# Operand addresses, whole-chunk 32-row products and a first expert without them, in a one-layer diffusion block with a mixture of experts

## The chip, the cores and the metric

The kernel runs on one core of one Trainium2 chip. TensorE (PE) multiplies matrices and loads its stationary operand by separate weight loads (PEld); VectorE (DVE), ScalarE (ACT) and GpSimd (POOL) work on elements; SyncE (SP) issues the large transfers. The metric is the time in device microseconds of one execution. It is compared with the time of the kernel before, as the median of several executions.

## The reference

One layer over 1024 latent tokens and 256 context tokens of width 1024. First a token mixer (a gated MLP over chunks of 128 tokens and a gated linear attention, fed by one input projection, merged and projected out), then a mixture of 16 experts, of which each token takes 2 out of one group of 4. Cut to what matters here:

```python
def moe_ffn(h, w_router, b_router, w_g, w_u, w_d):
    logits = h.astype(jnp.float32) @ w_router.astype(jnp.float32) + b_router.astype(jnp.float32)
    probs = jax.nn.softmax(logits, axis=-1).reshape(n_tok, N_EXPERT_GROUPS, EXPERTS_PER_GROUP)
    group_score = lax.top_k(probs, TOP_K)[0].sum(-1)
    g_sel = jnp.argmax(group_score, axis=-1)
    in_group = jnp.take_along_axis(probs, g_sel[:, None, None], axis=1)[:, 0]
    top_w, top_i = lax.top_k(in_group, TOP_K)
    weight = top_w / jnp.sum(top_w, axis=-1, keepdims=True)
    expert = (g_sel[:, None] * EXPERTS_PER_GROUP + top_i).reshape(-1).astype(jnp.int32)
```

Each expert computes (silu(h w_g) * (h w_u)) w_d on its tokens, with an inner width of 1536; the result, times the token's weight and a gate, is added to the stream, and a last RMSNorm follows. The inputs and weights are fp32.

## The kernel before

**Products.** An fp32 product is made from three fp32r ones: each operand is split into a high part (a copy rounded by ScalarE) and a low part (the rest, by VectorE), and hi·hi, hi·lo and lo·hi are added up in PSUM. So a matmul of 128x128 by 512 columns appears three times, with names ending in h and l.

**Stages.** The input projection (mm<-hxh,wh and the like, L256), the attention, the gate and branch projections (mm<-gbh and mm<-zh, L256), the output projection (L994), the router, and from about 1160 us on the experts.

**Experts.** The experts are handled in an order sorted by their counts, in 16 slots; RANK tells which of the sorted experts stands in which slot, and the first slot always holds expert 0. Each slot has room for 128 tokens in the block "a" and for 32 times UNITS[slot] tokens more in the block "b". An expert has 18 weight pages of 1 MB: three chunks of 4 for gate and up (w_gu) and 6 for down (w_d). load() has SP bring a page into one of ten raw buffers; part() has ScalarE and VectorE split it into one of three hl buffers; block_a() runs 12 matmuls of 512 columns per page from hl, with the stationary xah, xal (the tokens, transposed) or aah, aal (the activations). block_b() uses the raw fp32 page and 32 stationary columns, four products side by side in the array, for two pages at a time: 16 instructions with one unit, 32 with two. They are recorded as twice as many. After each chunk silu and a product on ScalarE and VectorE make sa (and sb_ for block b), PE transposes them (aat, abt), and split_a() makes aah and aal.

**Around the experts.** own_rows() finds the tokens of the first expert, and its rows are gathered by POOL as soon as they are known. places() works out the tokens of all other slots, on VectorE, behind the first chunk of the first expert. The rows of the next expert are gathered in the second chunk. At the end of a slot ya (and yb) is added to the stream in memory by an indirect transfer of POOL (put). In the last slot, tail() fetches finished rows (fetched, tile fx) and normalises them (normed, tile fq) while the last expert runs. If an expert has more tokens than its slot has room for, a loop behind the last slot handles the rest in blocks (overflow_block), with the expert's pages loaded again.

**Order.** Each engine works through its instructions in a fixed order. The program's scheduler sets it from the order of the code and from issue_after, which lets instructions be issued only behind a named one.

Of the kernel before, what the change touches and what calls it, by code (L numbers as in the profile page):

```python
# [18 lines left out]
S = 1024  # L19
D = 1024  # L20
CT = 256
E = 16
# [31 lines left out]
UNITS = tuple(2 if r == 1 else 1 if r < 10 else 0 for r in RANK)  # L54
# [24 lines left out]
def constants():  # L79
    p = np.arange(128)  # L80
    s, t = p[:, None], p[None, :]
    f = np.concatenate([
        np.eye(128),
        np.ones((128, 128)),
        (s < t) * 1.0,
        (s % 32) == np.arange(2),
    ], 1).astype(np.float32)
    t64 = np.arange(64)[None, :]
    i = np.concatenate([
        (s % 64) <= t64, (s % 64) >= t64,  # L90
        2 * (s + 128 * (np.arange(16) // 2)[None, :]) + (np.arange(16) % 2)[None, :],
        np.broadcast_to(2 * (S + np.arange(CAP) % TRASH)[:, None], (CAP, 16)).reshape(128, 144),
    ], 1).astype(np.int32)
# [12 lines left out]
    sl[:, 3] = 15 - e + 65536 * (e == 0)  # L106
    c = np.arange(128)[None, :]
    g4, r = s // 32, s % 32
    trash = np.concatenate([S + s, 4 * (S + 128 + r) + g4, 4 * (S + 160 + r) + g4], 1)
    z = np.concatenate([  # L110
        np.broadcast_to(16 * np.concatenate([c, 128 + c % 32, 160 + c % 32], 1), (128, 384)),
        np.broadcast_to([[32, 128, 128]], (128, 3)), np.broadcast_to([[1, 4, 4]], (128, 3)),
        np.concatenate([0 * s, g4, g4], 1) - trash, trash,
        np.stack([s // 32 + 4 * np.arange(8)[None], np.broadcast_to(s % 32, (128, 8)), np.ones((128, 8)),
                  np.zeros((128, 8))], 2).reshape(128, 32),
    ], 1).astype(np.float32)
    return f, i, g.reshape(128, 96), ((s - t) % 32 == 0).astype(np.float32), z, sl.reshape(128, 64)
# [48 lines left out]
def body(tc, A, out):  # L166
# [39 lines left out]
    sil = cp.tile([128, 8, 2], F32, name="sil")  # L206

# [737 lines left out]
    tk0, ch0 = (cp.tile([128, 3], I32, name=n) for n in ("tk0", "ch0"))  # L945
# [27 lines left out]
    kz = t1.tile([128, 428], F32, name="kz")  # L973
# [11 lines left out]
    V.tensor_copy(tri.rearrange("p i c -> p (i c)"), kz[:, 396:428])  # L985
# [142 lines left out]
    def own_row(i):  # L1128

        R = st_[i][5]  # L1130
        V.tensor_scalar(own[:, i, :], kz[:, 0:384], R[:, 7, 0:1], R[:, 5, 0:1], op0=ALU.is_equal, op1=ALU.mult)
        V.tensor_copy(tri[:, i, 3:4], R[:, 4, 0:1])

    def own_rows():

        p = ax("own")
        for b in range(3):
            for i in range(8):
                PE.matmul(p[:, 4 * b:4 * b + 4], own[:, i, 128 * b:128 * b + 128], tri[:, i, :], start=i == 0,
                          stop=i == 7)  # L1140
        f = t1.tile([128, 3, 4], F32, name="f3")
        V.tensor_copy(f.rearrange("p b c -> p (b c)"), p[:, 0:12])
        for c in range(3):
            V.tensor_mul(f[:, :, c], f[:, :, c], kz[:, 384 + 3 * c:387 + 3 * c])
        V.tensor_add(f[:, :, 0], f[:, :, 0], f[:, :, 1])
        V.tensor_add(f[:, :, 2], f[:, :, 2], kz[:, 393:396])
        V.tensor_add(f[:, :, 0], f[:, :, 0], f[:, :, 2])
        placed.append(V.tensor_copy(tk0, f[:, :, 0]))
        V.tensor_copy(ch0, f[:, :, 3])
# [10 lines left out]
    raws, ready = [], []  # L1160
# [17 lines left out]
    def load():  # L1178
        raws.append(page_tile([128, 2048]))
        e, n, i = order.pop(0)  # L1180
        return SP.dma_start(raws[-1], A[n][bass.ds(expert(e), 1), i].rearrange("o p n -> (o p) n") if e else A[n][0, i])

    def part():
        raw = raws.pop(0)
        hl = split_tile()
        SC.activation(hl[:, 0, :], raw, AF.Copy)  # L1186
        V.tensor_sub(hl[:, 1, :], raw, hl[:, 0, :].bitcast(F32))  # L1187
        ready.append(tuple(a.rearrange("p (k n) -> p k n", k=2) for a in (raw, hl[:, 0, :], hl[:, 1, :])))

    def page():  # L1190
        if not ready:
            if not raws:
                load()
            part()
        return ready.pop(0)
# [84 lines left out]
    with tc.issue_after(counted.ins), tc.issue_after(scaled.ins):  # L1280
        for i in range(2):
            part()
# [61 lines left out]
    x1_quarter = x1_d.rearrange("t (g c) -> (t g) c", g=4)  # L1344
    zf = ep_.tile([128, 512], F32, name="zf", tag="fq", bufs=FQB)
# [14 lines left out]
    def block_a(acc, st, k0, pg, start, stop):  # L1360

        _, wh, wl = pg
        for k in range(2):
            for n, (x, w) in enumerate(((0, wh), (0, wl), (1, wh))):
                for h in range(2):
                    PE.matmul(acc[h], st[x][:, k0 + k, :], w[:, k, 512 * h:512 * h + 512],  # L1366
                              start=start and (k, n) == (0, 0), stop=stop and (k, n) == (1, 2))

    def block_b(n, acc, st, k0, pgs, first, last):

        if n > 1 and first:
            PE.matmul(acc, zz[:, 0:128], zz, start=True, stop=False)
        for i, (w, _, _) in enumerate(pgs):
            for j in range(n):
                for k in range(2):
                    end = last and (i, j, k) == (len(pgs) - 1, n - 1, 1)
                    for g in range(4):
                        PE.matmul(acc[32 * g:32 * g + 32, 256 * j:256 * j + 256], st(j, k0 + 2 * i + k),
                                  w[:, k, 256 * g:256 * g + 256], start=n == 1 and first and (i, k) == (0, 0), stop=end,
                                  tile_position=(0, 32 * g))  # L1380
# [165 lines left out]
    wAB = prep_a(0, *first_xa, ch0[:, 0:1]), prep_b(0, first_xb[0], lambda j: ch0[:, j + 1:j + 2])  # L1546
    before = []
    for e in range(E):
        U = UNITS[e]
        for c in range(3):  # L1550
            pa, pb = [pt(f"pa{h}", "pa", 4) for h in range(2)], pt("pb", "pb", 2) if U else None
            for i in range(0, 4, 2):
                pgs = [page() for k in range(2)]
                first = e + c + i == 0
                if not first:
                    block_b(U, pb, xb_, 2 * i, pgs, i == 0, i == 2)
                for k in range(2):
                    block_a(pa, XA, 2 * (i + k), pgs[k], i + k == 0, i + k == 3)
                if first:
                    block_b(U, pb, xb_, 2 * i, pgs, i == 0, i == 2)  # L1560
            if U:
                sb_ = ep_.tile([128, 2, 128], F32, name="sb_", bufs=2)
                pv = pb.rearrange("p (j u n) -> p j u n", j=2, u=2)[:, 0:U]
                SC.activation(sb_[:, 0:U], pv[:, :, 0], AF.Silu)
                V.tensor_mul(sb_[:, 0:U], sb_[:, 0:U], pv[:, :, 1])
            p = pt("aat", "pt", 2)
            for h in range(2):
                sa = ep_.tile([128, 2, 128], F32, name="sa", bufs=4)
                pv = pa[h].rearrange("p (g u n) -> p g u n", g=2, u=2)
                SC.activation(sa, pv[:, :, 0], AF.Silu)  # L1570
                mul = V.tensor_mul(sa, sa, pv[:, :, 1])
                for k in range(2):
                    PE.transpose(p[:, 256 * h + 128 * k:256 * h + 128 * k + 128], sa[:, k, :], ident)
            split_a(p, aah[:, 4 * c:4 * c + 4, :], aal[:, 4 * c:4 * c + 4, :])
            if U:
# [3 lines left out]
                SC.activation(abT[:, c, 0:U].rearrange("p j t -> p (j t)"), p[:, 0:128 * U], AF.Copy)  # L1579
            if c == 0:  # L1580
# [10 lines left out]
        for i in range(0, 6, 2):  # L1591
            pgs = [page() for k in range(2)]
            block_b(U, pb, ab_, 2 * i, pgs, i == 0, i == 4)
            for k in range(2):
# [54 lines left out]
    ep_.release()  # L1649
    cp.release()  # L1650
# [15 lines left out]
```

## Time and profile before

| | us |
|---|---|
| median of 3 executions | 2281.84 |
| lowest and highest | 2281.76, 2284.72 |
| the profiled execution | 2284.32 |
| its span, first to last instruction | 2282.5 |
| PE, DVE, ACT, POOL busy | 2207.9, 1417.8, 1059.9, 205.0 |

The span is the time that the trace covers; 1.8 us of the profiled execution lie around it. The mean granted clock of TensorE was 0.985 of full speed. Busy time is a union of the intervals in which an engine's instructions ran; a matmul's record is longer than the distance to the next one's start, because matmuls overlap.

### The profile page before, as it was taken

Reading aid. Unit: us, or ns where it says so; the run is one execution under the profiler, and the core shown is the slowest. Engines: PE = TensorE matmul, PEld = TensorE weight load, DVE = VectorE, ACT = ScalarE, POOL = GpSimd, SP = SyncE. Lnnn points to the kernel's source line nnn. Section 1 sums busy time; section 2 is a strip of 40 time slices with the busy share of each in tenths; the row PEclk is TensorE's granted clock in tenths of the full one; section 3 lists DMA queues with packets and bytes.
Section 4 is the critical chain, followed back from the end, with each engine's and each line's share of the span. In section 5 each row is a group of like instructions: output and inputs, shape, how many; then the busy total and the mean of one; then the engine's idle time right before and its main releaser. Section 6 shows DMA issues by size and latency. Waiting matters only on the chain. (4 is left out here: it accounts for less than half of the span.)

```text
span 2282.5 us, 36688 instructions
## 1 busy us (share of the span) xinstructions
PE 2207.9 (97%) x14595; PEld 1785.5 (78%) x14596; DVE 1417.8 (62%) x2135; ACT 1059.9 (46%) x1334; POOL 205.0 (9%) x176
## 2 busy tenths in 40 slices
PE   9999999999999999999969999999999999999975
PEld 6999898888889978888957677777777777777654
DVE  5644215846762354246877568786868687666667
ACT  3312125534542153233235456665757565555554
POOL 0011000000000000001331110000101010100031
PEclk9999999999999999999979999999999999999988
DMA  7665433656741366445658679797979798877774
GB/s 291 195 207 170 154 128 105 195 179 194 233 169 59 116 220 225 157 129 204 186 194 304 228 279 347 285 362 289 366 283 375 288 348 303 288 278 278 261 254 161
DMA packets 141986, 530.06 MB, mean 232 GB/s; under 512 B 17159, under 2 KB 57919, under 8 KB 94705
## 3 DMA queue, kind: packets, MB, share of 16 engines
q1 hardware_dynamic: 119584, 467.97, 56.2%
q0 software_dynamic: 21072, 55.43, 8.8%
q10 hardware_dynamic: 1152, 4.26, 0.5%
q8 instruction: 116, 1.90, 0.3%
q14 instruction: 62, 0.50, 0.1%
HBM read 457.36 MB, written 70.44 MB: 231 GB/s over the span
## 5 line engine op out<-in xcount | busy, mean ns | idle before, releaser
L1187 DVE TENSOR_TENSOR hl<-praw,hl 128x2048 fp32r<-128x2048 f32 x174 | 402.0, 2313 | 157.6 <-ACT hl L1186 155.1
L1366 PE MATMUL pa<-hl,xah 128*128 128x512 f32 x1536 | 437.1, 403 | 16.1 <-ACT hl L1186 11.4
L1186 ACT ACTIVATE hl<-praw 128x2048 fp32r<-128x2048 f32 x174 | 333.1, 1915 | 206.2 <-PE pa L1366 206.1
L1366 PEld LDWEIGHTS pa<-hl,xah 128*128 128x128 f32 x1536 | 284.7, 189 | 98.4 <-issue 17.3
L1187 DVE TENSOR_TENSOR hl<-raw,hl 128x2048 fp32r<-128x2048 f32 x114 | 261.0, 2291 | 114.4 <-ACT hl L1186 113.0
L1186 ACT ACTIVATE hl<-raw 128x2048 fp32r<-128x2048 f32 x114 | 218.4, 1916 | 139.2 <-PE pa L1366 135.1
L1366 PE MATMUL pa<-hl,xal 128*128 128x512 f32 x768 | 243.1, 397 | 0.0
L1366 PE MATMUL pa<-hl,aah 128*128 128x512 f32 x768 | 219.3, 403 | 5.7 <-DVE hl L1187 4.5
L256 PE MATMUL mm<-wh,hxh 128*128 128x256 f32 (+1 forms) x768 | 218.3, 284 | 4.6 <-DVE vv L285 3.5
L256 PE MATMUL mm<-wl,hxh 128*128 128x256 f32 (+1 forms) x768 | 216.6, 282 | 0.0
L256 PE MATMUL mm<-wh,hxl 128*128 128x256 f32 (+1 forms) x768 | 215.8, 281 | 0.0
L256 PE MATMUL mm<-hxh,wh 128*128 128x512 f32 x448 | 178.7, 399 | 0.0
L256 PE MATMUL mm<-hxh,wl 128*128 128x512 f32 x448 | 178.6, 399 | 0.0
L256 PE MATMUL mm<-hxl,wh 128*128 128x512 f32 x448 | 178.4, 398 | 0.0
L1366 PEld LDWEIGHTS pa<-hl,aah 128*128 128x128 f32 x768 | 141.8, 189 | 45.5 <-DVE hl L1187 5.4
L1366 PEld LDWEIGHTS pa<-hl,xal 128*128 128x128 f32 x768 | 144.1, 189 | 34.3
L256 PEld LDWEIGHTS mm<-wh,hxh 128*128 128x128 f32 x768 | 145.2, 189 | 5.6 <-DVE vv L285 3.8
L256 PEld LDWEIGHTS mm<-wl,hxh 128*128 128x128 f32 x768 | 145.3, 189 | 0.0
L256 PEld LDWEIGHTS mm<-wh,hxl 128*128 128x128 f32 x768 | 145.0, 189 | 0.0
L238 DVE TENSOR_TENSOR wl<-wraw,wh 128x2048 fp32r<-128x2048 f32 (+1 forms) x36 | 82.7, 2298 | 100.1 <-ACT wh L237 78.8
L1366 PE MATMUL pa<-hl,aal 128*128 128x512 f32 x384 | 121.6, 398 | 0.0
L237 ACT ACTIVATE wh<-wraw 128x2048 fp32r<-128x2048 f32 (+1 forms) x36 | 69.1, 1918 | 69.9 <-PE mm L256 67.7
(503 smaller groups left out, 3623.4 us busy)
## 6 DMA issues: line engine op xcount, KB each, us to landing
praw<-in_w_gu_dram SPq DMA_DIRECT2D x116, 1024.0 KB, 6.8
raw<-in_w_gu_dram SPq DMA_DIRECT2D x76, 1024.0 KB, 7.2
praw<-in_w_d_dram SPq DMA_DIRECT2D x58, 1024.0 KB, 8.1
raw<-in_w_d_dram SPq DMA_DIRECT2D x38, 1024.0 KB, 7.5
wraw<-in_w_in_dram SPq DMA_DIRECT2D x24, 1024.0 KB, 4.8
wraw<-in_w_mod_dram SPq DMA_DIRECT2D x18, 1024.0 KB, 5.7
vb<-v_d POOLq DMA_DIRECT2D x16, 1024.0 KB, 6.8
xt<-in_x_dram SPq DMA_DIRECT2D x16, 512.0 KB, 5.7
```

The source lines that it names most:

```text
L237: SC.activation(wh[:, :n], raw[:, :n], AF.Copy)
L238: V.tensor_sub(wl[:, :n], raw[:, :n], wh[:, :n].bitcast(F32))
L256: end = PE.matmul(acc, Wst[a](k), Wmv[b](k), start=n == 0, stop=n == tot - 1)
L1186: SC.activation(hl[:, 0, :], raw, AF.Copy)
L1187: V.tensor_sub(hl[:, 1, :], raw, hl[:, 0, :].bitcast(F32))
L1366: PE.matmul(acc[h], st[x][:, k0 + k, :], w[:, k, 512 * h:512 * h + 512], start=start and (k, n) == (0, 0), stop=stop and (k, n) == (1, 2))
```

## The change

It has three parts. Three unused tiles (pad_l, pad_r, pad_e) move the tiles behind them in SBUF. The first slot has no block "b": UNITS[0] is 0, so own_rows() looks for 128 rows instead of 384, and no second gather is made for it. And block_b() runs for a whole chunk at once, four pages in gate/up and three in down, ahead of block_a(); the transposes of a chunk (turned_a) are issued behind the next chunk's block_b(), or behind the first page's block_a() in slots without units; pages are split when block_a() asks for them, while block_b() takes raw pages ahead.

```diff
-UNITS = tuple(2 if r == 1 else 1 if r < 10 else 0 for r in RANK)
+UNITS = tuple(0 if r == 0 else 2 if r == 1 else 1 if r < 10 else 0 for r in RANK)
...
+    cp.tile([128, 16], F32, name="pad_l")
+    rp = tc.alloc_tile_pool(name="rp", bufs=1, side="right")
+    rp.tile([128, 24], F32, name="pad_r")
...
-    own = t1.tile([128, 8, 384], BF16, name="own")
+    own = t1.tile([128, 8, 128], BF16, name="own")
...
-        for b in range(3):
-            for i in range(8):
-                PE.matmul(p[:, 4 * b:4 * b + 4], own[:, i, 128 * b:128 * b + 128], tri[:, i, :], start=i == 0,
-                          stop=i == 7)
+        for i in range(8):
+            PE.matmul(p[:, 0:4], own[:, i, :], tri[:, i, :], start=i == 0, stop=i == 7)
...
-    first_xb = gather_b(0, lambda j: tk0[:, j + 1:j + 2])
-    with tc.issue_after(first_xb[1][-1].ins):
+    with tc.issue_after(first_xa[1].ins):
         scatter(7)
...
+    ep_.tile([128, 24], F32, name="pad_e")
...
+    def turned_a(c, sas, sb_, U, behind):
+
+        with tc.issue_after(behind.ins):
             p = pt("aat", "pt", 2)
-            for h in range(2):
...
+            for k in range(4):
+                PE.transpose(p[:, 128 * k:128 * k + 128], sas[k // 2][:, k % 2, :], ident)
             split_a(p, aah[:, 4 * c:4 * c + 4, :], aal[:, 4 * c:4 * c + 4, :])
...
+    for e in range(E):
+        U = UNITS[e]
+        left = None
+        for c in range(3):
+            pa, pb = [pt(f"pa{h}", "pa", 4) for h in range(2)], pt("pb", "pb", 2) if U else None
+            if U:
+                end = block_b(U, pb, xb_, 0, raw_pages(4), True, True)
+                if left:
+                    turned_a(*left, end)
+            for k in range(4):
+                end = block_a(pa, XA, 2 * k, page(), k == 0, k == 3)
+                if k == 0 and left and not U:
+                    turned_a(*left, end)
...
-        for i in range(0, 6, 2):
-            pgs = [page() for k in range(2)]
-            block_b(U, pb, ab_, 2 * i, pgs, i == 0, i == 4)
-            for k in range(2):
-                block_a(pa, AA, 2 * (i + k), pgs[k], i + k == 0, i + k == 5)
-            if i == 2 and e + 1 < E:
-                wAB = prep(e + 1, *nxt)
-            if e + 1 == E:
-                tail(f"d{i}")
+        for i in range(0, 6, 3):
+            if U:
+                end = block_b(U, pb, ab_, 2 * i, raw_pages(3), i == 0, i == 3)
+                if i == 0:
+                    turned_a(*left, end)
+            if i == 3 and e + 1 < E:
+                wAB = prep(e + 1, *nxt)
+            for k in range(i, i + 3):
+                end = block_a(pa, AA, 2 * k, page(), k == 0, k == 5)
+                if k == 0 and not U:
+                    turned_a(*left, end)
+                if e + 1 == E and k % 2:
+                    tail(f"d{k - 1}")
```

The order on PE at the beginning of the third gate/up chunk of the fourth slot, which has one unit: pb is block b's product, pa are block a's, aat and abt the transposes of the chunk before. Before:

```order
L1378 MATMUL pb<-raw,xbT 32x256 x16
L1573 MATMUL aat<-kf,sa 128x128 x2
L1578 MATMUL abt<-kf,sb__13367 128x128
L1366 MATMUL pa_13388<-hl,xah 128x512
L1573 MATMUL aat<-kf,sa 128x128 x2
L1366 MATMUL pa_13389<-hl,xah 128x512
```

The same place after the change:

```order
L1385 MATMUL pb<-raw,xbT 32x256 x32
L1562 MATMUL aat<-kf,sa 128x128 x4
L1567 MATMUL abt<-kf,sb__13178 128x128
L1372 MATMUL pa_13189<-hl,xah 128x512
L1372 MATMUL pa_13190<-hl,xah 128x512
```

Before, 16 products of block b alternate with 24 of block a; now 32 stand ahead of all 48 of block a, and all five transposes stand right behind them.

The order on VectorE in the first expert after its first chunk, where L1311 to L1347 are places(), hl the low halves of pages and sa the activations. Before:

```order
L1187 TENSOR_TENSOR hl<-praw,hl 128x2048
L1325 TENSOR_TENSOR w_11565<-sel,fi 128x256
L1332 CAST ids<-fo 128x48
L1571 TENSOR_TENSOR sa<-sa,pa_11632 128x256
L1326 TENSOR_REDUCE fo<-w_11565 128x16
```

After the change:

```order
L1322 TENSOR_TENSOR sel<-ks,rank 128x256
L1193 TENSOR_TENSOR hl<-praw,hl 128x2048
L1330 TENSOR_TENSOR w_11498<-sel,fi 128x256
L1427 TENSOR_TENSOR aal<-aat,aah 128x512
L1331 TENSOR_REDUCE fo<-w_11498 128x16
L1193 TENSOR_TENSOR hl<-praw,hl 128x2048
```

In both, the instructions of places() alternate with the low halves; in the order after the change they also stand ahead of and behind aal of the first chunk.

The order on ScalarE in the last expert behind its first chunk, where fq is the squared sum of a finished row block and hl the high half of a page. Before:

```order
L1570 ACTIVATE sa<-pa_19071 128x256
L1509 ACTIVATE fq,fs<-fx 128x1024
L1418 ACTIVATE aah<-aat 128x512
L1509 ACTIVATE fq,fs<-fx 128x1024
L1186 ACTIVATE hl<-raw 128x2048
```

After the change:

```order
L1592 ACTIVATE sa<-pa_18882 128x256
L1517 ACTIVATE fq,fs<-fx 128x1024 x2
L1192 ACTIVATE hl<-raw 128x2048
L1521 ACTIVATE fx<-fx,fs 128x1024 x2
L1192 ACTIVATE hl<-praw 128x2048
```

The two fq stay ahead of the next page's high half; aah, which stood between them, has moved behind further pages.

## Rows read from the trace of the kernel before

**Rows 1.** The page, first part: busy us, share of the span, instructions, by engine.

```profile
PE 2207.9 (97%) x14595; PEld 1785.5 (78%) x14596; DVE 1417.8 (62%) x2135; ACT 1059.9 (46%) x1334; POOL 205.0 (9%) x176
```

**Rows 2.** Windows: PE, PEld, DVE, ACT, POOL busy (records), PEclk, DMA share, GB/s.

```profile
692.00:780.00 88.00, 88.00 (x749) 88.00 (x748) 23.18 (x42) 20.39 (x42) 0.00 (x0) 1.00 0.17 58
1160.00:1185.00 25.00, 8.63 (x69) 6.80 (x68) 21.40 (x87) 9.25 (x11) 13.10 (x9) 0.52 0.50 164
1185.00:1260.00 75.00, 74.98 (x595) 52.57 (x594) 53.86 (x76) 42.77 (x38) 6.55 (x5) 1.00 0.73 268
1346.00:1401.00 55.00, 55.00 (x273) 43.39 (x271) 50.04 (x36) 40.66 (x31) 5.49 (x2) 1.00 0.96 371
```

**Rows 3.** PE's waits: us in total, times, longest us.

```profile
PE pa L1366 <- ACT hl L1186: 12.5, 2, 11.4
PE pa L1366 <- DVE hl L1187: 9.1, 6, 3.9
```

**Rows 4.** Timeline of PE in slot 14 (down): start, us, engine, line, operation, count.

```profile
2166.00 0.63 PE L1366 MATMUL pa<-hl,aal 128*128 128x512 f32 x2
2166.55 1.93 PE L1378 MATMUL pb<-praw,abT 128*32 128x256 f32 x32
2168.42 1.19 PE L1366 MATMUL pa<-hl,aah 128*128 128x512 f32 x4
2169.45 0.61 PE L1366 MATMUL pa<-hl,aal 128*128 128x512 f32 x2
...
2170.80 0.61 PE L1366 MATMUL pa<-hl,aal 128*128 128x512 f32 x2
2171.26 1.10 PE L1366 MATMUL pa<-hl,aah 128*128 128x512 f32 x4
...
2172.67 1.10 PE L1366 MATMUL pa<-hl,aah 128*128 128x512 f32 x4
```

**Rows 5.** Lines of VectorE, 1201.5 to 1219.4: busy us, mean ns, idle before.

```profile
L1187 DVE TENSOR_TENSOR hl<-praw,hl 128x2048 fp32r<-128x2048 f32 x5 | 11.4, 2278 | 0.4 <-ACT hl L1186 0.4
L1325 DVE TENSOR_TENSOR w<-sel,fi 128x256 f32<-128x256 f32 x5 | 2.1, 413 | 0.0
L1326 DVE TENSOR_REDUCE fo<-w 128x16 f32<-128x256 f32 x5 | 2.1, 411 | 0.1
L1571 DVE TENSOR_TENSOR sa<-sa,pa 128x256 f32<-128x256 f32 x3 | 1.2, 409 | 0.0
...
L1419 DVE TENSOR_TENSOR aal<-aat,aah 128x512 fp32r<-128x512 f32 x1 | 0.7, 691 | 0.0
```

**Rows 6.** Timeline of PE in slot 1, which has two units.

```profile
1265.70 3.66 PE L1378 MATMUL pb<-praw,xbT 128*32 128x256 f32 x64
1269.29 1.19 PE L1366 MATMUL pa<-hl,xah 128*128 128x512 f32 x4
```

**Rows 7.** Timeline of PE in the branch projections, every twelfth start.

```profile
872.64 0.39 PE L256 MATMUL mm<-zh,wh 128*128 128x512 f32 x1
...
875.36 0.39 PE L256 MATMUL mm<-zh,wh 128*128 128x512 f32 x1
...
984.90 0.40 PE L256 MATMUL mm<-gbh,wh 128*128 128x512 f32 x1
...
987.70 0.40 PE L256 MATMUL mm<-gbh,wh 128*128 128x512 f32 x1
```

**Rows 8.** Timeline of POOL and PE at the start of the experts.

```profile
1175.90 2.34 POOL L1267 DMA_INDIRECT xa<-h_d,tk  x1 [4.61 <-DVE cf L1254]
...
1181.71 1.97 PE L1395 MATMUL xat<-kf,xa 128*128 128x128 f32 x8 [7.78 <-DMA xa<-h_d,tk]
```

**Rows 9.** Timeline of POOL, ACT and PE in the last expert.

```profile
2185.84 3.36 POOL L1422 DMA_INDIRECT x_d<-ya,tks  x1 [3.88 <-DVE ya L1612]
...
2202.20 1.06 ACT L1509 ACTIVATE fq<-fx 128x1024 bf16<-128x1024 f32 x1 [7.84 <-DMA fx<-x_d]
...
2206.72 1.22 PE L1366 MATMUL pa<-hl,xah 128*128 128x512 f32 x2 [11.36 <-ACT hl L1186]
```

More of the change, by code (lines that the diff above doesn't have):

```diff
@@ L944, in body @@
     more = cp.tile([1, 9, 16], I32, name="more")
-    tk0, ch0 = (cp.tile([128, 3], I32, name=n) for n in ("tk0", "ch0"))
+    tk0, ch0 = (cp.tile([128, 1], I32, name=n) for n in ("tk0", "ch0"))
     tok = cp.tile([128, 16], I32, name="tok")
@@ L1136, in own_rows @@
         p = ax("own")
[L1137 to L1149 removed]
+        for i in range(8):
+            PE.matmul(p[:, 0:4], own[:, i, :], tri[:, i, :], start=i == 0, stop=i == 7)
+        f = t1.tile([128, 4], F32, name="f3")
+        V.tensor_mul(f[:, 0:3], p[:, 0:3], kz[:, 128:131])
+        V.tensor_copy(f[:, 3:4], p[:, 3:4])
+        V.tensor_add(f[:, 0:1], f[:, 0:1], f[:, 1:2])
+        V.tensor_add(f[:, 2:3], f[:, 2:3], kz[:, 131:132])
+        V.tensor_add(f[:, 0:1], f[:, 0:1], f[:, 2:3])
+        placed.append(V.tensor_copy(tk0, f[:, 0:1]))
+        V.tensor_copy(ch0, f[:, 3:4])
     def scatter(i):
@@ L1159, in body @@
     order = [(e, n, i) for e in range(E) for n, k in (("w_gu", 12), ("w_d", 6)) for i in range(k)]
-    raws, ready = [], []
+    pages = []
     used = [0, 0]
@@ L1178, in load, with raw_pages, part @@
     def load():
-        raws.append(page_tile([128, 2048]))
         e, n, i = order.pop(0)
[L1181 to L1188, printed above, removed]
-    def page():
[L1191 to L1195, printed above, removed]
+        raw = page_tile([128, 2048])
+        pages.append([raw, None])
+        return SP.dma_start(raw, A[n][bass.ds(expert(e), 1), i].rearrange("o p n -> (o p) n") if e else A[n][0, i])
+    def raw_pages(n):
+        while len(pages) < n:
+            load()
+        return [p[0].rearrange("p (k n) -> p k n", k=2) for p in pages[:n]]
+    def part(i):
+        raw, hl = pages[i]
+        if hl is None:
+            hl = split_tile()
+            SC.activation(hl[:, 0, :], raw, AF.Copy)
+            V.tensor_sub(hl[:, 1, :], raw, hl[:, 0, :].bitcast(F32))
+            pages[i][1] = hl
+        return hl
+    def page():
+        raw_pages(1)
+        hl = part(0)
+        pages.pop(0)
+        return tuple(hl[:, j, :].rearrange("p (k n) -> p k n", k=2) for j in range(2))
     for i in range(8):
@@ L1365, in block_a @@
                 for h in range(2):
-                    PE.matmul(acc[h], st[x][:, k0 + k, :], w[:, k, 512 * h:512 * h + 512],
-                              start=start and (k, n) == (0, 0), stop=stop and (k, n) == (1, 2))
+                    end = PE.matmul(acc[h], st[x][:, k0 + k, :], w[:, k, 512 * h:512 * h + 512],
+                                    start=start and (k, n) == (0, 0), stop=stop and (k, n) == (1, 2))
+        return end
     def block_b(n, acc, st, k0, pgs, first, last):
@@ L1372, in block_b @@
             PE.matmul(acc, zz[:, 0:128], zz, start=True, stop=False)
-        for i, (w, _, _) in enumerate(pgs):
+        for i, w in enumerate(pgs):
             for j in range(n):
                 for k in range(2):
-                    end = last and (i, j, k) == (len(pgs) - 1, n - 1, 1)
+                    stop = last and (i, j, k) == (len(pgs) - 1, n - 1, 1)
                     for g in range(4):
-                        PE.matmul(acc[32 * g:32 * g + 32, 256 * j:256 * j + 256], st(j, k0 + 2 * i + k),
-                                  w[:, k, 256 * g:256 * g + 256], start=n == 1 and first and (i, k) == (0, 0), stop=end,
-                                  tile_position=(0, 32 * g))
+                        end = PE.matmul(acc[32 * g:32 * g + 32, 256 * j:256 * j + 256], st(j, k0 + 2 * i + k),
+                                        w[:, k, 256 * g:256 * g + 256], start=n == 1 and first and (i, k) == (0, 0),
+                                        stop=stop, tile_position=(0, 32 * g))
+        return end
     def weight(x, ch, name):
@@ L1545, in body @@
     gf = xg = None
-    wAB = prep_a(0, *first_xa, ch0[:, 0:1]), prep_b(0, first_xb[0], lambda j: ch0[:, j + 1:j + 2])
+    wAB = prep_a(0, *first_xa, ch0), []
     before = []
[L1548 to L1552, printed above, removed]
-                pgs = [page() for k in range(2)]
-                first = e + c + i == 0
-                if not first:
-                    block_b(U, pb, xb_, 2 * i, pgs, i == 0, i == 2)
-                for k in range(2):
[L1558 to L1565, printed above, removed]
-            p = pt("aat", "pt", 2)
-            for h in range(2):
[L1568 to L1573, printed above, removed]
+    def turned_a(c, sas, sb_, U, behind):
+        with tc.issue_after(behind.ins):
+            p = pt("aat", "pt", 2)
+            for k in range(4):
+                PE.transpose(p[:, 128 * k:128 * k + 128], sas[k // 2][:, k % 2, :], ident)
             split_a(p, aah[:, 4 * c:4 * c + 4, :], aal[:, 4 * c:4 * c + 4, :])
@@ L1579, in body @@
                 SC.activation(abT[:, c, 0:U].rearrange("p j t -> p (j t)"), p[:, 0:128 * U], AF.Copy)
+    for e in range(E):
[12 more added lines that the diff above has]
+            if U:
+                sb_ = ep_.tile([128, 2, 128], F32, name="sb_", bufs=2)
+                pv = pb.rearrange("p (j u n) -> p j u n", j=2, u=2)[:, 0:U]
+                SC.activation(sb_[:, 0:U], pv[:, :, 0], AF.Silu)
+                V.tensor_mul(sb_[:, 0:U], sb_[:, 0:U], pv[:, :, 1])
+            sas = []
+            for h in range(2):
+                sa = ep_.tile([128, 2, 128], F32, name="sa", bufs=4)
+                pv = pa[h].rearrange("p (g u n) -> p g u n", g=2, u=2)
+                SC.activation(sa, pv[:, :, 0], AF.Silu)
+                mul = V.tensor_mul(sa, sa, pv[:, :, 1])
+                sas.append(sa)
+            left = c, sas, sb_ if U else None, U
             if c == 0:
@@ L1649, in body @@
     ep_.release()
+    rp.release()
     cp.release()
```

19 lines of the change are left out of this document (7 added, 12 removed).

## The prediction, written before the result was known

> **What bounds the kernel now.** I read the page first: TensorE is busy 97% of the span, VectorE 62%, ScalarE 46% [rows 1]. Next the table by stage: in the input projection PE is busy in all of 88.0 us, and in the experts in 74.98 of 75.0 and 55.00 of 55.0 us, at clock 1.00 [rows 2]. Then PE's list of waits: of 2282.5 us it waited 12.5 for ScalarE's hi halves of pages and 9.1 for VectorE's lo halves [rows 3]. So the time is the number of matmul records times the time from one start to the next, plus a few waits at the ends of stages. A change pays only if it takes records away, or shortens that distance, or shortens one of those waits; it costs if it makes PE wait where it now does not. "Busy, mean ns" cannot be used for the distance, because matmuls overlap; I take it from starts in the timeline.
>
> **1. First expert without 32-row products.** The block of 32 records starts at 2166.55, the next block_a at 2168.42: 1.87 us. The aal pair at 2166.00 should be followed after a third of a page's 1.40 per six, 0.47, but the block starts after 0.55, so 0.08 is lost ahead; the four aah behind it take 1.03 to the next pair, not two thirds of 1.40, so 0.10 is lost behind [rows 4]. One block costs 2.05 us. The first expert has 9 (6 in gate/up, 3 in down): −18.5, and five transposes at about 0.11 less: **−19**.
> What this uncovers: the 18 pages of one expert cost VectorE 18 × 2.28 = 41.0 us, the products sa and halves aal 3 × (0.82 + 0.69) = 4.5, the next expert's xal and the output ya 2.8 (estimate, four 128x512 passes at aal's price), and in the first expert also places(), some 7 us, of which the two largest groups are 2.1 + 2.1 [rows 5]: 55 us. PE has 18 pages at 2.72 (twelve aligned matmuls, below) and 20 transposes: 51 us. Until now nine blocks, 18 us, hid places(). The excess is 4; the order puts places() between the lo halves that PE waits for, so three buffers of split pages do not cover all of it; PE works in order, and what it waits for there delays every page behind. I take **+5**, bounds 0 (the buffers cover it) and +8 (nothing covers it).
> Other experts without 32-row products, 7 of 16 less the first, run like the stretch with 50.04 us of VectorE in 55.0 and DMA share 0.96 [rows 2]: no stall there now, and about 1.2 us less PE time per expert later. Chaining the pages through three buffers I find no PE wait; bounds 0 to +8 for all six.
>
> **2. Whole chunk at once.** With two units 64 records take 1265.70 to 1269.29, 3.59 us [rows 6], against 1.87 for 32: 1.72 per 32 records, so 0.15 is fixed inside a block, and with 0.08 and 0.10 a block costs 0.33 whatever its length. Nine experts with units go from 9 blocks to 5: 9 × 4 × 0.33 = **−12**. Bounds −7 (only the 0.18 around it is saved, 36 × 0.18) and −14. The delayed transposes cost no PE time: they stand behind the next 32-row run (3.6 us in gate/up, 2.7 in down) which covers the silu and the product that they wait for; in experts without units they stand behind the first page's 2.7 us. The raw pages are needed earlier by up to three pages; VectorE's and ScalarE's halves are not. Loads are issued more than 20 us ahead, so no wait.
>
> **3. Addresses.** In the built programs of before, hl stands at 96 bytes modulo 128 on two of three pages and at 0 on the third; xah and xal at 64, aah and aal at 0, hx and gb at 64, wh, wl and zh at 96; of after, all of these at 0. Timeline, twelve starts of 512 columns each: zh with wh (both at 96) 872.64 to 875.36, 2.72 us or 226.7 ns; gb with wh (64 and 96) 984.90 to 987.70, 2.80 us or 233.3 ns [rows 7]. Same shape, type, line and clock. In the experts, six with hl and aa both at 0 take 2169.45 to 2170.80, 1.35; six on the next page (96 and 0) 2171.26 to 2172.67, 1.41 [rows 4]. So 512-column matmuls go at about 227 if both operands have the same remainder and 233 if not. In after both are 0. Expert stage, slots 0 to 14: 3240 matmuls from a mean of 232.8 to 227: −18.5. First stages: 1728 of 512 columns (hx 1344, gb 384) by 6.6: −11.4. With 256 columns the sign is against the change: 749 records in 88 us, 117.5 ns, with 96 and 64 [rows 2], while the output projection with equal remainders shows about 120: 1536 × 2.4 = +3.7, and +0.9 elsewhere. Together **−25** (−18.5 and −6.8), bounds 0 (the remainder is not the cause) and −31.
> The Trainium skill speaks against this term: "TensorE: Matmul & The Clock Gate", section "Step-by-step: what each phase is for", gives the weights and the moving data independent read ports, by which a relation between the two addresses could not matter and this term would be 0; "SBUF — State Buffer", section "Operand start alignment", states start addresses as a matter of legality and untimed. The rows disagree with the first so far.
>
> **4. Start of the experts.** The own row is 128 instead of 384 wide and the chain behind it has fewer passes; the rows of the first expert are gathered after it, and PE waits 7.78 us for them [rows 8]: **−0.8** (0 to −1.5).
>
> **5. Tail.** In the last expert ScalarE must first take fx, which landed at 2202.20 after the add of ya that POOL issued at 2185.84; only then comes page 5's hi half, and PE waits 11.36 us [rows 9]. The changed order keeps both fq ahead of that page, as the fence on ScalarE in the change shows, so the chain starts at the end of slot 14 as before: **0**, bounds −5 and +5 (the low clock after the wait, 0.52 over 1160 to 1185 in the other place with such a wait [rows 2], may last shorter or longer).
>
> **Sum.** −19 + 5 − 12 − 25 − 1 + 0 = −52. The profiled run took 2284.3, so 2232; it lies 2.5 above the median of its runs, so **2230**.
>
> **Rivals.** *Alignment gives nothing* (the page's rule above; the cause of 233 is a property of the tile, not of the remainder): parts 1, 2, 4 alone, 2282 − 27 = 2255. For it: before has no row with both at 0 except in short runs. Against: two stages show the same 6 to 7 ns. *VectorE or the page DMA become the bound in the seven experts without units*: their PE time falls by 1.2 us each, VectorE is at 50 of 55, and the pages would have to come at 383 GB/s where 371 at share 0.96 is shown [rows 2]. If neither follows, alignment is lost there (8) and the first expert's stall is 8, not 5: 2241. *The clock falls in the long 32-row runs*: PE at clock 1.00 is shown through 3.59 us of them; only slot 1 gets longer ones (7 us). If each of its five brought a low clock for as long as the run itself, +15: 2245; it ends above before only if the whole of that slot, 86 us, ran at half speed, which no row suggests as PE has no wait there. *On the other side*: the first expert now has room for 128 tokens instead of 160. The reference's routing gives it 124 for these inputs. At 129 the overflow loop after the last expert would load its 18 pages again, 18.9 MB at 371 GB/s, 51 us, serially with the products, and a second final normalisation: at least +60, so 2290 or more. It decides at 128 tokens. *The change does not do what it says*: then 2280.
>
> **Chances.** Forecast as summed 0.60; alignment nothing 0.18; bound in experts without units 0.10; clock 0.05; overflow or another slower ending 0.04; nothing 0.03. Low end: every free bound (−5 stall, −6 alignment, −5 tail, −2 chunks) is 2212; high end takes in the alignment rival with 3 for its stalls: 2258. A measurement of this kernel tells 0.2%, 4.6 us, from no change; all cases but the last two are far below, so faster 0.93, same 0.03, slower 0.04.
>
> **What would show it.** Starts of pa pairs at 1.36 per six on every page, in slots with and without units; three 32-row runs per expert in gate/up of 3.6 us and two of 2.7; gb and hx at 226 to 227; 256 columns at 120 rather than 117.5; PE waits on VectorE's hl of some 5 us near the first expert's second chunk; the first expert about 52 to 56 us long; the wait in the last expert again 11 us. It is wrong if pages keep 1.41 per six, if PE waits for DMA of a page, or if the clock of a stage that was at 1.00 is lower.

## The result and the profile after

The kernel after takes 2251.36 us (median of 4), the kernel before 2283.28 in the same comparison: ratio 0.9854, interval 0.9841 to 0.9868. So 32 us went, where 52 were forecast.

The page's first part and PE's list of waits (us in total, times, longest us), kernel after:

```profile
PE 2170.6 (96%) x14286; PEld 1787.4 (79%) x14287; DVE 1415.1 (63%) x2127; ACT 1056.9 (47%) x1327; POOL 213.0 (9%) x174
```

```profile
PE pa L1372 <- ACT hl L1192: 14.5, 2, 13.2
PE pa L1372 <- DVE hl L1193: 10.6, 6, 5.0
PE xat L1403 <- DMA xa<-h_d,tk: 9.7, 1, 9.7
PE pos L1117 <- DVE R L1100: 6.5, 1, 6.5
PE xat L1403 <- DMA xa<-h_d,tks: 2.7, 1, 2.7
```

Against [rows 1, 3] PE's busy time fell by 37 us while its waits grew: ScalarE's halves 12.5 to 14.5, VectorE's 9.1 to 10.6, and a new wait of 2.7 us for the rows of the second expert (tks). Where the span went can be cut at the first block_a matmul of slots 0, 2 and 15, which have no 32-row product ahead of them in the kernel after. The lengths are differences of those starts in PE's timeline (216 block_a matmuls per slot), here for all kernels of this study, with the ratio of their timed runs to the kernel before:

| kernel | first start | slots 0, 1 | slots 2 to 14 | slot 15 | ratio (interval) |
|---|---|---|---|---|---|
| before | 1183.5 | 162.7 | 836.4 | 81.6 | 1 |
| after | 1180.8 | 146.8 | 820.6 | 83.5 | 0.9854 (0.9841 to 0.9868) |
| a_pads | 1181.4 | 164.0 | 836.1 | 83.4 | 1.000 (0.9987 to 1.0014) |
| b_first | 1181.1 | 151.1 | 836.3 | 82.1 | 0.9929 (0.9914 to 0.9943) |
| c_chunk | 1178.3 | 158.8 | 824.1 | 82.7 | 0.9915 (0.9898 to 0.9931) |
| f_pads256 | 1174.1 | 162.2 | 826.8 | 83.2 | 0.9934 (0.9916 to 0.9951) |
| e_after256 | 1177.9 | 146.3 | 809.9 | 82.8 | 0.9779 (0.976 to 0.9798) |
| g_ends | 1181.7 | 141.8 | 809.9 | 71.0 | 0.9729 (0.9711 to 0.9747) |
| h_ends2 | 1173.4 | 142.4 | 809.9 | 77.9 | 0.9745 (0.9732 to 0.9758) |

Of the 32.7 us between the two profiled spans, slots 0 and 1 gave 15.9 (forecast 17.8: −19 + 5, slot 1's share of the whole chunks and both slots' shares of the addresses), slots 2 to 14 gave 15.8 (forecast 26.6: eight experts at 1.32 and thirteen at 1.23), the stages ahead 2.7 (forecast 7.6), and the last slot and the end cost 1.6 (forecast 0). The repeated runs of the kernel before, below, show that such a difference ahead of the experts can come without any change. More than half of the shortfall is in slots 2 to 14, where PE's lists show no wait in either kernel: it is in the matmuls themselves. Timeline of PE, kernel after, slot 14:

```profile
2118.43 0.63 PE L1372 MATMUL pa<-hl,xal 128*128 128x512 f32 x2
...
2119.83 0.63 PE L1372 MATMUL pa<-hl,xal 128*128 128x512 f32 x2
...
2122.62 0.61 PE L1372 MATMUL pa<-hl,xal 128*128 128x512 f32 x2
...
2123.98 0.61 PE L1372 MATMUL pa<-hl,xal 128*128 128x512 f32 x2
2124.53 1.93 PE L1385 MATMUL pb<-raw,abT 128*32 128x256 f32 x32
2126.28 1.05 PE L1385 MATMUL pb<-praw,abT 128*32 128x256 f32 x16
2127.25 0.65 PE L1562 MATMUL aat<-kf,sa 128*128 128x128 f32 x4
```

Six matmuls take 1.36 on the last page of the chunk and still 1.40 on the two pages ahead of it, all with their operands at multiples of 128 bytes. The 48 records of three pages run in one go, 2124.53 to 2127.25. And gb with wh, every twelfth start, which answers to [rows 7], the kernel after:

```profile
980.84 0.40 PE L256 MATMUL mm<-gbh,wh 128*128 128x512 f32 x1
...
983.64 0.40 PE L256 MATMUL mm<-gbh,wh 128*128 128x512 f32 x1
```

2.80 us, the same as before; the forecast was 2.72.

### The profile page after: what moved, and what is told of

It is laid out like the page before. It is cut to its first block, busy times and chain, and to the rows that moved or that the text cites. A ratio compares the mean times of both kernels' runs of the same rounds, so it can differ in the third digit from the quotient of the medians.

```text
span 2249.8 us, 36046 instructions
## 1 busy us (share of the span) xinstructions
PE 2170.6 (96%) x14286; PEld 1787.4 (79%) x14287; DVE 1415.1 (63%) x2127; ACT 1056.9 (47%) x1327; POOL 213.0 (9%) x174
## 5 line engine op out<-in xcount | busy, mean ns | idle before, releaser
L1372 PE MATMUL pa<-hl,xah 128*128 128x512 f32 x1536 | 428.1, 399 | 19.8 <-ACT hl L1192 13.2
L1372 PE MATMUL pa<-hl,aah 128*128 128x512 f32 x768 | 214.8, 401 | 6.3 <-DVE hl L1193 5.0
L238 DVE TENSOR_TENSOR wl<-wraw,wh 128x2048 fp32r<-128x2048 f32 (+1 forms) x36 | 82.7, 2298 | 99.7 <-ACT wh L237 99.6
```

Source lines behind the costliest of these rows:

```text
L238: V.tensor_sub(wl[:, :n], raw[:, :n], wh[:, :n].bitcast(F32))
L1372: end = PE.matmul(acc[h], st[x][:, k0 + k, :], w[:, k, 512 * h:512 * h + 512], start=start and (k, n) == (0, 0), stop=stop and (k, n) == ( ...
```

## Experiments

**Addresses by themselves.** Two kernels hold only one tile over nearly all of SBUF, filled with zeros, and runs of 16 to 48 fp32r matmuls from chosen places in it, with no other engine at work:

```diff
+    def run(m, s, n, cols):
+        p = acc[cnt[0] % 4]
+        cnt[0] += 1
+        for k in range(n):
+            PE.matmul(p[:, 0:cols], big[:, s + 128 * (k % 4):s + 128 * (k % 4) + 128], big[:, m:m + cols],
+                      start=k == 0, stop=k == n - 1)
```

> Leaves out the whole computation: one tile over nearly all of SBUF, filled with zeros, and runs of fp32r matmuls from chosen byte offsets in it, moving operand and stationary operand apart, with nothing else running; the output is zeros. Theory of the prediction (equal remainders modulo 128 give 227 ns per 512-column matmul, others 233): every pair of offsets in the 14 by 14 table has remainder 0 for both, so all 196 show 227, and in the second part the remainders alone decide. Theory of placement, formed from the trace after the change: 227 only where both operands lie in the same part of SBUF as well, 232 to 233 where one lies low and one high whatever the remainders; the table then has two fast blocks and two slow ones, with the edge somewhere between byte 85,000 and 113,000. A third possibility, distance between the operands (edge near 91,000 bytes), gives a fast band along the diagonal and not two blocks. If the address plays no part and other engines' traffic does, all are 227 or less.

All 196 pairs of places take 227 ns (mean of start-to-start times from the trace), low or high in SBUF, near or far: placement and distance are out. In the second part, where only remainders differ, 227 stands on the diagonal and mostly 233 off it (229 where the moving operand is 64 bytes ahead), for each of four pairs of places. So the address relation is real, with nothing else running. But then the kernel after should have had 227 everywhere, and a finer step was needed: all offsets in the first map lay at multiples of 512 or within 96 bytes of one, so no pair differed by 128.

> As the first map, leaving out the whole computation: moving and stationary operand each from offsets of 0 to 480 bytes in steps of 32 behind a multiple of 512, 512 columns and then 256. Theory of the prediction (modulo 128): a matmul of 512 columns takes 227 ns wherever the two remainders modulo 128 agree, so on four diagonals of the 16 by 16 table. New theory (modulo 256), from the addresses in the program after the change (hx and gb at 0, w at 128 modulo 256: 233; zh and w both at 128: 227): 227 on two diagonals only, 233 where the operands differ by 128. With 256 columns the other way round: about 120 on the fast diagonals, 117 elsewhere.

Mean ns from start to start, worked out from the trace's starts without the two distances at the beginning of a run and the one at its end. Columns: stationary operand at 0, 32, ... 480 bytes; rows: moving operand at 0 and at 128, with 512 columns and then, for 0, with 256:

```
512, moving at   0: 227 227 227 230 233 233 229 233 227 233 233 234 232 233 229 233
512, moving at 128: 233 233 229 233 227 233 233 234 232 233 229 233 227 233 233 234
256, moving at   0: 119 118 118 117 119 120 118 117 120 118 118 117 119 120 118 117
```

The pattern repeats every 256 bytes and shifts with the moving operand. Over all 16 rows, 227 stands where the two differ by a multiple of 256 (29 of 32 such entries, three show 229), 232 to 233 where they differ by 128, 229 where the moving one is 64 ahead. (In the first row the entries at 32, 64 and 96 stand alone: they are among the first runs of that kernel, and in the other rows the same differences give 233 to 234.) With 256 columns the small difference is the other way round, 119 to 120 at equal remainders and 117 to 120 elsewhere.

**Pads alone, as in the change, and modulo 256.**

```diff
+    cp.tile([128, 16], F32, name="pad_l")
+    rp = tc.alloc_tile_pool(name="rp", bufs=1, side="right")
+    rp.tile([128, 24], F32, name="pad_r")
...
+    ep_.tile([128, 24], F32, name="pad_e")
```

> The kernel before with the three pads alone, the rest untouched. Theory of the prediction (equal remainders give 227 ns): 25 us less, about 2258, ratio 0.989. Theory of placement: of the expert stage only the pages whose split buffer lies near the stationary operands gain, some 72 of 216 matmuls per expert by about 3 ns, 0.2 to 0.35 us per expert, and the first stages nothing: 3 to 5 us less, ratio 0.998 to 0.9985. If the wait of 3 us for a store in the attention's input, gone in the profile after, comes from the addresses too, up to 8.

Ratio 1.000 (0.9987 to 1.0014): nothing. In the first stages the operands stand as in the kernel after, and gb with wh keeps its 2.80 per twelve. The first stages thus speak against the rule modulo 128. The expert stage is no clean test of it: aah and the near hl page (the one whose buffer lies beside the stationary operands) stand at 32 modulo 128 and xah at 0, since the unchanged tiles ahead of them are longer. What the near page gains in the kernel after is therefore not in this run.

In f_pads256 hx, gb, z, w, hl and the stationary operands all stand at 0 modulo 256:

```diff
-    rp.tile([128, 24], F32, name="pad_r")
+    rp.tile([128, 56], F32, name="pad_r")
...
-    ep_.tile([128, 24], F32, name="pad_e")
+    ep_.tile([128, 16], F32, name="pad_e")
```

> The kernel before with pads alone, chosen so that hx, gb, z, w, all hl, xah, xal, aah and aal stand at 0 modulo 256. Modulo 256: first stages 1728 times 6.6 ns, 11.4 us less, 4.5 more for the 256-column matmuls, expert stage 3240 times 5.6, 18 less: 25 us less, ratio 0.989. Modulo 128 (the prediction), after the pads of the change gave nothing: no gain, ratio 1.0.

Ratio 0.9934 (0.9916 to 0.9951), 15 us, and 9.6 of them in slots 2 to 14. Timeline of PE, f_pads256, every twelfth start:

```profile
982.16 0.39 PE L260 MATMUL mm<-gbh,wh 128*128 128x512 f32 x1
...
984.88 0.39 PE L260 MATMUL mm<-gbh,wh 128*128 128x512 f32 x1
```

2.72: here is the forecast's 227. The forecast's 25 was still too large. In slot 2 the distances between block_a matmuls sum to 47.56 us instead of 48.61, 1.05 of the forecast 1.23; those at the transposes grew by 0.36 (0.66 to 0.82 between aat, 1.65 to 1.85 ahead of them), so that the slot got only 0.60 shorter. In the kernel after, where the transposes stand in one group of four, this loss does not appear: from c_chunk to e_after256, below, the slots 2 to 14 get 14.2 shorter, and the transposes keep their distances.

**The kernel after, moved to 0 modulo 256.**

```diff
-    rp.tile([128, 24], F32, name="pad_r")
+    rp.tile([128, 56], F32, name="pad_r")
```

> The kernel after with 128 bytes more in the right-hand pad, so that w, z and the far hl pages move from 128 to 0 modulo 256 like the rest. Modulo 256: 11.4 less in the first stages, 1 more for 256 columns, 3240 times 4.6 ns, 15 less, in the experts: 25 us less than the kernel after, ratio to the kernel before about 0.975. Modulo 128: the same time as the kernel after, 0.985. If VectorE or the page loads bind in experts without 32-row products, 8 of the 15 are lost: 0.978.

Ratio to the kernel before 0.9779 (0.976 to 0.9798): 50 us less than before, 17 less than the kernel after. Slots 2 to 14 go from 820.6 to 809.9. Timeline of PE, e_after256, slot 14:

```profile
2105.94 0.61 PE L1372 MATMUL pa<-hl,xal 128*128 128x512 f32 x2
...
2107.30 0.61 PE L1372 MATMUL pa<-hl,xal 128*128 128x512 f32 x2
...
2108.66 0.61 PE L1372 MATMUL pa<-hl,xal 128*128 128x512 f32 x2
...
2110.02 0.61 PE L1372 MATMUL pa<-hl,xal 128*128 128x512 f32 x2
```

1.36 for six on every page, not only on one in three. The branch projection:

```profile
980.68 0.39 PE L256 MATMUL mm<-gbh,wh 128*128 128x512 f32 x1
...
983.40 0.39 PE L256 MATMUL mm<-gbh,wh 128*128 128x512 f32 x1
```

2.72 here too. The ratio is near the 0.978 that was expected if VectorE or the page loads took part of the gain back, but that did not happen: PE's list has no wait between 1330 and 2130 us. Slots 2, 4, 6, 8 and 10 shorten by 0.7 each against the kernel after, those with products by 0.9. The expected 15 us in the experts counted all 3240 matmuls, but only two pages of three moved: in slot 2 the distances between block_a matmuls fell by 0.78 us, which makes 11.7 in 15 slots, and slots 0 to 14 gave 11.2.

**The first expert alone.** UNITS[0] = 0, own rows 128 wide, no second gather; two-page blocks as before. The addresses are nearly as before: as less stands ahead of them, aah and the near hl page move from 128 to 96 modulo 256. They stay equal to each other and unequal to the rest, and slots 2 to 14 take 836.3 against 836.4.

```diff
-UNITS = tuple(2 if r == 1 else 1 if r < 10 else 0 for r in RANK)
+UNITS = tuple(0 if r == 0 else 2 if r == 1 else 1 if r < 10 else 0 for r in RANK)
```

> The kernel before with no 32-row products for the first expert, own rows 128 wide; addresses and the two-page blocks as before. By the prediction's terms 19 less, 5 more for places() uncovered and 0.8 less at the start: 15 less, ratio 0.9935. By the trace after the change: the same 19, but waits of 1.9 on lo halves, 3 on the gather of the second expert's rows with a low clock behind it (1.5), and 1.3 more, not 0.8 less, at the start: 11 to 12 less, ratio 0.995.

Ratio 0.9929 (0.9914 to 0.9943), 16 us. Of the 14.0 us between the two profiled spans 11.6 lie in slots 0 and 1, and the rest ahead of the experts, where executions of one program differ by as much (see the repeated runs of before, below). So the timed ratio is that of the first line of the expectation, and the slots are near the second, 11 to 12.

**Whole chunks alone,** with the moved transposes. In the first expert's first chunk block b stands behind the second page.

```diff
-            for i in range(0, 4, 2):
-                pgs = [page() for k in range(2)]
...
+            if U and e + c:
+                end = block_b(U, pb, xb_, 0, raw_pages(4), True, True)
```

> The kernel before with the 32-row products for a whole chunk at once and the delayed transposes, also in the first expert (there the first chunk's block stands behind the second page, since its rows arrive late); addresses as before. By the prediction's terms 0.33 us per block, 4 blocks less in ten experts: 13 less, ratio 0.9943. Rival: what was lost of the forecast in the middle experts was lost here, the fixed cost of a block being only the 0.18 around it: 7 less, ratio 0.997.

Ratio 0.9915 (0.9898 to 0.9931), 19 us. In the slots it is 3.9 (two experts) and 12.3 (eight): 1.6 per expert, 0.40 for each block saved instead of 0.33, so the rival of 0.18 per block is out. That the moved transposes gave part of it in every expert is out too: slot 2, which has no block b, takes 53.19 in both kernels when the next expert's first block (1.55 and 3.28 between its first and last record) is taken off. Another 5 us of its profile lie ahead of the experts, where this edit changes nothing.

**The kernel before again, twice.**

> The kernel before, unchanged, once more. With whole chunks at once 19 us went where the blocks account for 13; in the profiles 6 of these lie at 125 to 170 us, in the input stage, which that change does not touch. If that stretch varies from execution to execution, this profile shows it up to 6 us shorter than the first one did, with everything behind it shifted by as much; if it is a property of the program, it takes the same as in the first profile.

> The same a third time, for the same question: the stretch from 125 to 170 us differs between these executions of one program by some us, or not at all.

The stretch 125 to 170 us of the kernel before, of its two further executions, and of c_chunk (windows: PE, PEld, DVE, ACT, POOL busy with records, PEclk, DMA share, GB/s), in this order:

```profile
125.00:170.00 45.00, 40.73 (x325) 39.98 (x324) 21.39 (x34) 6.95 (x15) 7.42 (x11) 0.96 0.63 191
```

```profile
125.00:170.00 45.00, 41.48 (x344) 40.73 (x343) 21.90 (x34) 7.38 (x17) 7.54 (x11) 1.00 0.64 190
```

```profile
125.00:170.00 45.00, 44.95 (x375) 44.41 (x375) 21.45 (x34) 7.22 (x15) 7.54 (x11) 1.00 0.70 215
```

```profile
125.00:170.00 45.00, 45.00 (x376) 44.50 (x375) 18.06 (x30) 6.83 (x14) 7.54 (x11) 1.00 0.68 208
```

One program has 325, 344 and 375 matmul records in the same 45 us: in some executions PE waits 3.5 us there for values whose buffer comes free only when a store (v_d) lands, in others not. The experts of the three begin at 1183.5, 1180.3 and 1179.0, while slots 2 to 14 differ by 0.1 us. What a profile shows ahead of the experts is thus no evidence of 5 us; the lengths by slot are. Executions that are alike in this stretch can be compared: e_after256 has the same wait of 3.5 as the first of the three, and its experts begin 5.7 sooner; h_ends2, below, has none, as the third, and its experts begin 5.6 sooner. The kernel after, with a wait of 0.6, begins them 1.9 later than the third: nothing was gained there.

**The two ends of the expert stage.** On top of e_after256, the normalisation of finished rows is queued on ScalarE behind the latest split page, and the second expert's rows are transposed two pages later:

```diff
+                with tc.issue_after(splits[-1].ins):
+                    normed(int(n[1]), gf)
...
+                if e == 0 and k == 4:
+                    wAB = prep(1, *nxt)
```

> As the run before it (all at 0 modulo 256), and two waits taken away: in the last expert the normalisation of finished rows is queued on ScalarE behind the split of page 12 and not ahead of page 5, and the second expert's rows are transposed two pages later in the first expert. If the waits of 13 and 2.7 us in the trace after are due to these places, they go, with some 5 and 1 us of low clock behind them: 20 us less than without, ratio 0.966. If the wait in the last expert only moves to the end (the normalised rows now leave last), 4 less, ratio 0.973.

Ratio 0.9729 (0.9711 to 0.9747): 62 us less than before, the lowest ratio here. Slots 0 and 1 get 4.5 us shorter than in e_after256, as the wait for the second expert's rows goes, and slot 15 gets 11.8 shorter. PE's waits in g_ends:

```profile
PE pa L1372 <- ACT hl L1192: 10.1, 2, 7.7
PE xat L1403 <- DMA xa<-h_d,tk: 9.5, 1, 9.5
PE pos L1117 <- DVE R L1100: 6.5, 1, 6.5
PE pa L1372 <- DVE hl L1193: 4.2, 5, 1.2
```

The wait of 13.4 that e_after256 has is gone from the list, one of 7.7 stays, and after the last block_a matmul the kernel takes 22.1 us instead of 17.9, since two normalisations now stand on VectorE ahead of the last product's output. The ratio of 0.973 that was expected if the wait only moved to the end came out for another reason: 11.8 us were gained in the slot, and 4.2 lost at the end. h_ends2 queues them earlier:

```diff
-TAIL = dict(g0=["f0", "f1"], g2=["g", "n0", "n1", "f2"], d0=["f3"], d2=["n2", "n3"])
+TAIL = dict(g0=["f0", "f1"], g1=["g", "n0", "f2"], g2=["n1", "f3"], d0=["n2", "n3"])
```

> As g_ends, with the four normalisations queued one chunk earlier each (the first behind page 8, the last before page 16), so that none stands on VectorE ahead of the last product's output. In g_ends the last matmul is followed by 22.1 us to the end, where 17.9 would do, and PE still waits 10 us for hi halves. If the late normalisations are the cause of both, 4 us at the end and 2 to 4 in the slot go: 2215, ratio 0.970. If the waits come from the rows' landing, the first normalisation now waits for it again and the time is that of g_ends, 0.973.

Ratio 0.9745 (0.9732 to 0.9758), no better, near the expectation's second line: the end is back at 17.8 us, but slot 15 takes 77.9 instead of 71.0, as PE then waits up to 7.3 us for a low half. The wait and the end trade against each other.

## Why the prediction was right in sign and too large

**Part 3, the step that failed.** It said that 512-column matmuls go at about 227 "if both operands have the same remainder and 233 if not", with remainders modulo 128. The map shows the period to be 256 bytes. In the kernel before, the pairs at 227 were z with w, both at 224 modulo 256, and the near hl with aah, both at 128; the slow ones differed by 32, 64 or 96. No pair differed by 128, so [rows 4, 7] fit both rules, and I took the smaller period without a row that spoke for it. The change put the tiles on the right (w, z, two of three hl) at 128 modulo 256 and those on the left (hx, gb, xah, aah, one hl) at 0. So the first stages gained nothing (2.80 per twelve), and in the experts only the near page did, in gate and up: 3.5 us in slots 2 to 14 (820.6 against c_chunk's 824.1), at that rate 0.5 in the first two. About 4 came of the 25. With 128 bytes more on the right 17 more came by the timed ratio. e_after256 is the kernel that this prediction had in mind: its median is 2234 where 2230 was forecast, and slots 0 to 14 gave 42.9 of the forecast 44.4. So the step that failed is the choice of 128, and less the size of the term: from c_chunk to e_after256 the addresses gave 14.2 us in slots 2 to 14, where 16.0 were forecast, and the whole chunks gave more than forecast.

The rival "alignment gives nothing" named 2255, close to the 2251 measured, but that is luck, as its reason is refuted: with nothing else running, moving one operand by 32 bytes changes the distance from 227 to 233. The Trainium skill, "TensorE: Matmul & The Clock Gate", section "Step-by-step: what each phase is for", would have the weights' and the data's read ports independent; the map does not agree with a reading by which their addresses can't matter to each other. Which part of the chip they meet in, no run here shows.

Of the small term within part 3, the 256-column matmuls, the sign held: in the first map they took 119.8 to 120.0 with both remainders equal, 116.7 with the moving operand at 96 and the stationary one at 64, and 117.8 at 0 and 64.

**Part 1** was right in its large term, and its second term was near by number and not by its mechanism. b_first has 11.6 of the forecast 14 in slots 0 and 1: 7.4 came back instead of 5, within the bound of 8. The place that was named, waits for lo halves while places() stands between them, made up little of it. Timeline of POOL and PE in the first expert, kernel after:

```profile
1209.68 0.73 PE L1372 MATMUL pa<-hl,xah 128*128 128x512 f32 x2 [0.39 <-DVE hl L1193]
...
1214.70 7.34 POOL L1273 DMA_INDIRECT xa<-h_d,tks  x1 [36.43 <-DVE rank L1346]
...
1216.77 0.73 PE L1372 MATMUL pa<-hl,xah 128*128 128x512 f32 x2 [0.77 <-DVE cnt L1347]
...
1230.47 1.75 PE L1403 MATMUL xat<-kf,xa 128*128 128x128 f32 x8 [2.70 <-DMA xa<-h_d,tks]
```

The same gather and transposes, kernel before:

```profile
1218.89 0.97 POOL L1267 DMA_INDIRECT xa<-h_d,tks  x1 [34.47 <-PE abt L1578]
```

```profile
1246.95 1.04 PE L1395 MATMUL xat<-kf,xa 128*128 128x128 f32 x8
```

PE waits little for VectorE (0.39, 0.77). It waits 2.70 for the second expert's rows, which POOL gathers when places() ends. Counted from the first block_a matmul, that gather is issued no later than before (33.9 us against 35.4). But PE comes to the transposes after 46.9 us instead of 63.4, as the blocks ahead are gone, and the gather lands 15.6 us after its issue instead of 6.7. Before, the rows lay ready for 21 us. Why the gather takes longer, 7.34 us on POOL instead of 0.97, no run here shows. The matmuls right behind the wait start 427 ns apart for some two us; the granted clock is 0.50 (1.2 GHz) from 1231.9 to 1233.7. g_ends, which moves the transposes back by two pages, took 4.5 us out of these slots.

**Part 2** was right: forecast 12 for nine experts; 16.2 for ten in c_chunk, 0.40 per block instead of 0.33, a little over its bound.

**Part 4** had the wrong sign. The token numbers come earlier, but PE's wait grew from 7.78 [rows 8] to 9.66, and from the last matmul of the output projection to the first transpose 25.6 us pass instead of 24.5. Timeline of POOL, SP and PE, kernel after:

```profile
1171.39 2.03 POOL L1273 DMA_INDIRECT xa<-h_d,tk  x1 [4.11 <-DMA h_d<-h]
1172.58 0.33 SPq L1179 DMA_DIRECT2D praw<-in_w_gu_dram  x1
...
1179.04 1.97 PE L1403 MATMUL xat<-kf,xa 128*128 128x128 f32 x8 [9.66 <-DMA xa<-h_d,tk]
```

The gather is now released by the last store of h_d, not by VectorE, and counted from that matmul it is issued 0.8 us sooner, as forecast. But SP asks for the next page, a megabyte, 1.2 us after it, probably because without block_b a raw page of the first expert is free as soon as it is split; and the gather takes 7.7 us from its issue to PE instead of 5.8. b_first, with the same first expert, waits 9.63; c_chunk, which keeps the first expert's block_b and asks for no page there, 7.61. All five kernels without that block take 7.5 to 7.9 us from issue to PE, the six with it 5.6 to 5.8. That the page load slows the gather is argued from this: no run moved the load alone. It was in none of the rows read.

**Part 5**: the order was read rightly and the wait stayed, 13.2 for 11.4, and 1.9 us more in slot 15, inside its bounds of 5. The timeline of the kernel after, answering to [rows 9]:

```profile
2151.57 3.36 POOL L1430 DMA_INDIRECT x_d<-ya,tks  x1 [7.49 <-DVE ya L1632]
...
2168.57 1.06 ACT L1517 ACTIVATE fq<-fx 128x1024 bf16<-128x1024 f32 x1 [8.57 <-DMA fx<-x_d]
...
2172.76 1.22 PE L1372 MATMUL pa<-hl,xah 128*128 128x512 f32 x2 [13.21 <-ACT hl L1192]
```

From the add to the first fq 17.0 us pass against 16.4, both fq stand ahead of the page as before, and PE comes to that page 8.0 us after the add instead of 9.5, so it waits longer. The other rivals did not occur: no wait for a page load, slots without units 0.3 shorter than in c_chunk rather than bound, and no slower records in the long 32-row runs of slot 1 (446 distances between them sum to 24.1 us, 54 ns each; before 504 to 27.9, 55 ns; granted clock 1.00 in both). The 383 GB/s in the rival of the page loads does not come out of its own 1.2 us (371 × 55.0 / 53.8 is 379); nothing hangs on it.

## What to carry to other kernels

Before a rule is read out of a few addresses, list the differences that the rows actually hold: a rule fitted to differences of 0, 32, 64 and 96 says nothing about 128, and a kernel of a few thousand matmuls with nothing else in it settles it in one run. When work that hid other work is removed, look not only at the engine that was hidden but at what it releases (here a gather by POOL, which also took longer), and at transfers that start sooner (here a page load right behind a gather, which may have slowed it). And compare traces stage by stage: one stretch of this kernel differs by 3 to 5 us between executions of one program, while thirteen experts repeat to 0.1 us.

## What the runs showed of the hardware

The distance between fp32r matmuls of 512 columns depends on the difference of the start addresses of moving and stationary operand modulo 256 bytes: 227 ns at 0, 229 where the moving operand is 64 bytes ahead, 232 to 234 at the others, with no other engine at work (d_map2); at equal addresses modulo 256 it was 227 for all 196 pairs of places in SBUF that were tried (d_map). With 256 columns equal remainders are not faster but up to 3 ns slower (119.5 against 116.7 where the moving operand is 32 bytes ahead). The gain of the right choice in this kernel is 17 us of 2251 (e_after256 against the kernel after).
